# Gates, convolutions, the trigonometric table and statistics behind weight preparation, and a second work queue for the gates

## Chip, cores and metric

The kernel runs on one core of a Trainium2 chip. The metric is the device time of one execution in microseconds; the number quoted is the median of three runs.

## What the reference computes

A trunk of two layers works on x of 256 rows and 2048 columns in float32. Every layer normalises x, multiplies it by a large input matrix, and runs two token mixers beside each other: an mLSTM with 4 heads, whose q and k go through a depthwise convolution of width 5, and a retention with 8 heads, whose q and k are rotated. Both are gated, projected, mixed and added to x.

```python
h = rmsnorm(x, norm_w)
proj = jnp.einsum('bsd,de->bse', h, w_in)
qk_m = jax.nn.silu(depthwise_conv(jnp.concatenate([q_m, k_m], axis=-1), conv_w, conv_b))
gates = (g_m + b_mgate).reshape(b, s, 4, NH_M)
h_m = mlstm_scan(q_m, k_m, v_m, gates[0], gates[1]) + flipped(...)
q_r = rope(q_r, cos, sin);  k_r = rope(k_r, cos, sin)
h_r = retention_scan(...) + flipped(...)
y = mix_m * (u_m @ w_proj_m) + mix_r * (u_r @ w_proj_r)
return x + y @ w_out
```

## The kernel before

**Matrix products.** Every operand in float32 is split into a high and a low part (`hi`, `lo`), and a product is three matmuls (`mm3`). A `gemm` makes a block of 512 columns (384 or 400 for the first four blocks of q and k) for both halves of the rows. It walks over the 2048 inner elements in 8 chunks; a chunk loads 512 KB of weights into a tile `raw` (7 of them), splits them (`wsplit`: `whi` by a cast on ScalarE, `wlo` by a subtraction on VectorE; 12 tiles, so six chunks) and issues 12 matmuls into two PSUM tiles.

**Order of the blocks in a layer.** Five blocks of q and k for the mLSTM (qk0 with the 16 gate columns, qk1, qk2, qk3 of 384 columns, qk4 of 512), four value blocks (here vm0 to vm3), eight blocks of the retention's q, k and v, then gated blocks and projections. From the third value block on, further products (`seven`) are worked off beside the blocks as "side items"; they need sums of the operand (`s_hi`, `s_lo`, made by `sums_of_operand`).

**Work between the chunks.** What follows a block is put into the list `pending` by `later`, and `gemm` calls `run_later` before each chunk from the second or third on, which takes one step of the list's first entry. Entries are generators that yield where a step ends:

- `conv_block`: transposes three or four columns blocks of q or k (PSUM tile `tr`), a ScalarE activation for the middle tap, four `scalar_tensor_tensor` on VectorE for the others (`conv`), a Silu, and the split into `qkm_hi` and `qkm_lo`.
- `mlstm_gates`: some ten small steps from `gates` to the log forget gates `lf` (Exp and Ln on ScalarE), sums along the rows by six small matmuls (`pc`), diagonal tiles `dg`, which for every head are broadcast by two matmuls (`pb`) and reduced to the weights `wt` and their row maxima.
- `late_setup` (layer 0 only): loads positions (`pos_i`), `freq` and `rp`, and makes the table of sines and cosines in about 90 VectorE steps of 128x128.
- `mlstm_matrix`, one per head: scores (`psc`), row sums, the scaled matrix `a_sb`, its transpose `at`; then `mlstm_out` (`po`).

**What sets the order on an engine.** The code's order is not that of the queues. A planner of the framework places each instruction by its position in the code less an offset, as soon as its inputs and its tiles are ready in the plan; each engine then runs its queue in that order. Weight loads and splits have an offset of `AHEAD` = 800 positions, and whatever goes through the wrappers `vec` and `sca` one of `URGENT` = 1600:

```python
vec, sca = Ahead(nc.vector), Ahead(nc.scalar)   # every call under high_priority(offset=URGENT)
```

Matmuls have none. In the profile all instructions that go through the wrappers have line 119.

**Tiles.** Tags share a number of tiles: PSUM 8 (`bank`), `t512` 7 (q/k blocks, `conv`, `dg`, `freq`, `ahi`, `a_sb` and others), `act` 8 (`wt`, the table's two `trig` tiles, `at`, the split value blocks `vm_hi` and `vm_lo`, the operand sums).

Of the kernel before, what the change touches and what calls it, by code (L numbers as in the profile page):

```python
# [61 lines left out]
def encoder_kernel(ctx: ExitStack, tc: tile.TileContext, x, x_t, positions, w_main, w_qk0, w_qk1, b_mgate, vecs, b_mix,  # L62
# [92 lines left out]
    def late_setup():  # L155
        pos_i = sm.tile([P, NT], I32, name="pos_i", bufs=1)
        with nc.allow_non_contiguous_dma(reason="256 positions onto partitions"):
            nc.sync.dma_start(out=pos_i, in_=positions.rearrange("b (t p) -> p (b t)", p=P))
        freq = t512("freq")[:, 0:64]
        nc.sync.dma_start(out=freq, in_=inv_freq.broadcast_to([P, 64]))  # L160
        rp = sm.tile([P, 8], F32, name="rp", bufs=1)
        nc.sync.dma_start(out=rp, in_=rpieces.broadcast_to([P, 8]))
        pos_f = sm.tile([P, NT], F32, name="pos_f", bufs=1)
        vec.tensor_copy(out=pos_f, in_=pos_i)

        scr = [actt("trig0"), actt("trig1")]
        used = []

        def trig(name):
            used.append(name)  # L170
            i, n = divmod(len(used) - 1, 8)
            return scr[i][:, n * NT * 64:(n + 1) * NT * 64]
        ang = trig("ang")
        for t in range(NT):
            vec.tensor_scalar(out=ang[:, t * 64:(t + 1) * 64], in0=freq, scalar1=pos_f[:, t:t + 1],
                                    scalar2=None, op0=ALU.mult)
        ahi = t512("ahi", F32R)[:, 0:NT * 64]
        vec.tensor_copy(out=ahi, in_=ang)
        ahf = ahi.bitcast(F32)
        alo = trig("alo")  # L180
        vec.tensor_tensor(out=alo, in0=ang, in1=ahf, op=ALU.subtract)
        acc = trig("acc")
        vec.memset(acc, 0.0)


        def drop_turns(v, magic):
            rnd = trig("rnd")
            vec.tensor_scalar(out=rnd, in0=v, scalar1=magic, scalar2=magic, op0=ALU.add, op1=ALU.subtract)
            vec.tensor_tensor(out=v, in0=v, in1=rnd, op=ALU.subtract)
        for k in range(4, -1, -1):  # L190
            for part in (alo, ahf):
                del used[3:]
                pr = trig("pr")
                vec.tensor_scalar(out=pr, in0=part, scalar1=rp[:, k:k + 1], scalar2=None, op0=ALU.mult)
                drop_turns(pr, 1.5 * 2 ** 25)
                drop_turns(pr, 1.5 * 2 ** 23)
                vec.tensor_tensor(out=acc, in0=acc, in1=pr, op=ALU.add)
                drop_turns(acc, 1.5 * 2 ** 23)
        lim = 0.49999997
        vec.tensor_scalar(out=acc, in0=acc, scalar1=lim, scalar2=-lim, op0=ALU.min, op1=ALU.max)  # L200
        red = trig("red")
        vec.tensor_scalar(out=red, in0=acc, scalar1=6.283185307179586, scalar2=None, op0=ALU.mult)
        sca.activation(out=sin_sb, in_=red, func=AF.Sin)
        neg = trig("neg")
        vec.tensor_scalar(out=neg, in0=red, scalar1=-1.0, scalar2=None, op0=ALU.mult)
        vec.tensor_tensor(out=neg, in0=neg, in1=red, op=ALU.min)
        vec.tensor_scalar(out=neg, in0=neg, scalar1=1.5707963267948966, scalar2=None, op0=ALU.add)
        sca.activation(out=cos_sb, in_=neg, func=AF.Sin)
# [170 lines left out]
    def sums_of_operand(ht_hi, ht_lo, make_items):  # L379
        s_hi, s_lo = bigt("s_hi", 2, F32R), bigt("s_lo", 3, F32R)  # L380

        def whole(dst, kt):
            ks = slice(kt * S, (kt + 4) * S)
            vec.tensor_tensor(out=dst, in0=ht_hi[:, ks].bitcast(F32), in1=ht_lo[:, ks].bitcast(F32), op=ALU.add)
            return dst.rearrange("p (k t x) -> p k t x", t=NT, x=P)
        for j in range(2):
            a0 = whole(actt("a0"), 4 * j)
            a1 = whole(actt("a1"), HK + 4 * j)
            yield
            sums = [actt("sa"), actt("sb")]  # L390
            f = [s.rearrange("p (i k x) -> p i k x", i=2, x=P)[:, i] for s in sums for i in range(2)]
            vec.tensor_tensor(out=f[0], in0=a0[:, :, 1, :], in1=a1[:, :, 1, :], op=ALU.subtract)
            vec.tensor_tensor(out=f[1], in0=f[0], in1=a0[:, :, 0, :], op=ALU.subtract)
            vec.tensor_tensor(out=f[2], in0=a0[:, :, 0, :], in1=a0[:, :, 1, :], op=ALU.subtract)
            vec.tensor_tensor(out=f[3], in0=a1[:, :, 0, :], in1=f[1], op=ALU.add)
# [111 lines left out]
    def mlstm_gates(gates, gate_out):  # L507
# [6 lines left out]
        for t in range(NT):  # L514
            vec.tensor_copy(out=fpre[:, t], in_=g4[:, t, :, 1, :])
            vec.tensor_copy(out=ipre[:, t], in_=g4[:, t, :, 0, :])
        e, u, lf = small("e"), small("u"), small("lf")
        vec.scalar_tensor_tensor(out=e, in0=fpre, scalar=-1.0, in1=fpre, op0=ALU.mult, op1=ALU.max)
        sca.activation(out=e, in_=e, func=AF.Exp, scale=-1.0)
        vec.tensor_scalar(out=u, in0=e, scalar1=1.0, scalar2=None, op0=ALU.add)  # L520
        sca.activation(out=lf, in_=u, func=AF.Ln)
        d1 = small("d1")
        vec.tensor_scalar(out=d1, in0=u, scalar1=-1.0, scalar2=None, op0=ALU.add)
        vec.tensor_tensor(out=d1, in0=e, in1=d1, op=ALU.subtract)
        vec.reciprocal(out=u, in_=u)
        vec.tensor_tensor(out=d1, in0=d1, in1=u, op=ALU.mult)
        vec.tensor_tensor(out=lf, in0=lf, in1=d1, op=ALU.add)
        vec.scalar_tensor_tensor(out=lf, in0=fpre, scalar=0.0, in1=lf, op0=ALU.min, op1=ALU.subtract)
# [11 lines left out]
        vec.tensor_copy(out=cum, in_=pcv)  # L540
        vec.tensor_tensor(out=rj, in0=ipre, in1=cum, op=ALU.subtract)
# [8 lines left out]
        vec.tensor_copy(out=rj_hi, in_=rj)  # L550
        vec.tensor_tensor(out=rj_lo, in0=rj, in1=rj_hi.bitcast(F32), op=ALU.subtract)
# [3 lines left out]
        def diagonals(h):  # L555
            dgs = []
            for part in (rj_hi.bitcast(F32), rj_lo):
                dg = t512("dg", F32R)
                r = part[:, :, :, h:h + 1].rearrange("p t d o -> p d t o").broadcast_to([P, 2, NT, P])
                vec.tensor_tensor(out=dg.rearrange("p (d t x) -> p d t x", d=2, t=NT), in0=eye, in1=r,  # L560
                                        op=ALU.mult)
                dgs.append(dg)
            return dgs
        dgs = diagonals(0)
        for h in range(NH_M):
# [7 lines left out]
            for d, t, off, j0, nj, mask in pieces:  # L573
                w_h = wts[h][:, off:off + nj * P]
                vec.tensor_tensor_reduce(out=w_h, in0=pb[:, d * S + j0 * P:d * S + (j0 + nj) * P], in1=mask,
                                               scale=1.0, scalar=0.0, op0=ALU.add, op1=ALU.max,
                                               accum_out=rmax[:, t, d, h:h + 1])
        vec.tensor_scalar(out=nrm, in0=rmax, scalar1=-1.0, scalar2=None, op0=ALU.mult)
        for h in range(NH_M):
            for d, t, off, j0, nj, mask in pieces:  # L580
                w_h = wts[h][:, off:off + nj * P]
                sca.activation(out=w_h, in_=w_h, func=AF.Exp, bias=nrm[:, t, d, h:h + 1])
        floor = small("floor")
        vec.tensor_tensor(out=floor, in0=cum, in1=rmax, op=ALU.add)
        sca.activation(out=floor, in_=floor, func=AF.Exp, scale=-1.0)
        vec.tensor_scalar(out=floor, in0=floor, scalar1=16.0, scalar2=None, op0=ALU.mult)
# [3 lines left out]
    def conv_block(l, ch0, nch, ev, qk_hi, qk_lo):  # L590
        for g in range(0, nch, 2):
# [8 lines left out]
            for k2 in range(ng):  # L600
# [153 lines left out]
    for l in range(DEPTH):  # L754
# [6 lines left out]
        for b in range(5):  # L761
            if b == 0:
                ps = gemm(xop, wqk(w_qk0[l], N_QK0), "qk", N_QK0,
                          **(dict(ahead=first_raw, before=first_chunks) if l == 0 else dict(lead=2)))
                if l == 0:
                    for c in range(NBLK):
                        for t in range(NT):
# [3 lines left out]
                            sca.activation(out=xc, in_=xc, func=AF.Square,  # L771
# [206 lines left out]
        if l < DEPTH - 1:  # L978
# [164 lines left out]
```

## Time and profile before

| what | value |
|---|---|
| median of three runs | 2217.68 us (2213.07, 2217.68, 2217.74) |
| profiled execution: its own time | 2213.89 us |
| profiled execution: span | 2212.1 us, 28345 instructions |
| TensorE matmul busy | 2163.4 us (98%) |
| VectorE busy | 1766.4 us (80%) |
| ScalarE busy | 1269.7 us (57%) |
| DMA | 505.66 MB, mean 229 GB/s |

The profile is one execution; its times run from the start of the span. PE is TensorE (matmuls), PEld its weight loads, DVE VectorE, ACT ScalarE, POOL GpSimd, SP the engine that issues most DMAs. A name such as `wlo<-raw,whi` gives the tile written and the tiles read, and L119 is a line of the kernel. "PEclk" is the granted clock of TensorE as a share of full speed. Matmuls overlap each other, so the step from one start to the next, not the duration, is what one costs.

### The profile page before, as it was taken

The numbers are of one execution on the slowest core, as the hardware profiler recorded it, in microseconds if no ns is written. First come the engines' busy times: TensorE is split into PE (matmuls) and PEld (weight loads), VectorE is DVE, ScalarE is ACT, GpSimd is POOL, SyncE is SP. The second block draws the span as 40 slices with busy tenths as digits, with TensorE's granted clock in tenths as the row PEclk, the third lists the DMA queues.
The fourth block names the chain that finished last, engine by engine and source line by source line (L and its number), as shares of the span: only waits on it lengthen the run. The fifth ranks groups of instructions, "written<-read, shape, count | busy, mean of one in ns | idle before, by whom it ended". The sixth has DMA issues, their size and how long they took to land.

```text
span 2212.1 us, 28345 instructions
## 1 busy us (share of the span) xinstructions
PE 2163.4 (98%) x10072; PEld 1823.8 (82%) x10072; DVE 1766.4 (80%) x2281; ACT 1269.7 (57%) x1573; POOL 58.1 (3%) x114
## 2 busy tenths in 40 slices
PE   7889999999999999999999999999999999999998
PEld 6778888888788888888899888888888888888887
DVE  6895898888899879865568768889889988898654
ACT  7644556565766556654557445555567755666443
POOL 0000000000000000000000000000000000000000
PEclk9999999999999999999999999999999999999999
DMA  7455567667778877786756456666777788777763
GB/s 269 138 187 162 190 222 234 226 226 235 245 258 272 294 257 257 231 302 206 232 157 211 152 176 210 229 227 230 235 234 260 259 277 273 263 250 264 268 202 125
DMA packets 156190, 505.66 MB, mean 229 GB/s; under 512 B 18960, under 2 KB 21264, under 8 KB 156048
## 3 DMA queue, kind: packets, MB, share of 16 engines
q1 hardware_dynamic: 140240, 464.00, 63.4%
q0 software_dynamic: 8320, 27.27, 3.1%
q10 hardware_dynamic: 7488, 12.59, 2.0%
q8 instruction: 79, 1.29, 0.2%
q14 instruction: 63, 0.52, 0.1%
HBM read 474.42 MB, written 29.36 MB: 228 GB/s over the span
## 4 chain that ended last, share of the span: by engine, by line
PE 91%; DVE 4%; DMA 2%; ACT 1%; issue 1%; SPq 0%; ACTq 0%; DVEq 0%
PE pj L271 5%; PE pj L269 5%; PE pj L270 5%; PE wo L271 3%; PE wo L270 3%; PE vr L269 3%; PE vr L270 3%; PE wo L269 3%; PE vr L271 3%; PE qr L269 3%; PE zr L269 3%; PE zr L271 3%; PE qr L271 3%; PE qr L270 3%; PE zr L270 3%; PE vm L269 2%
## 5 line engine op out<-in xcount | busy, mean ns | idle before, releaser
L260 ACT CAST whi<-raw 128x1024 fp32r<-128x1024 f32 (+2 forms) x824 | 842.5, 1035 | 635.7 <-PE pj L270 119.7
L261 DVE TENSOR_TENSOR wlo<-raw,whi 128x1024 fp32r<-128x1024 f32 (+2 forms) x824 | 974.1, 1200 | 280.0 <-ACT whi L260 250.1
L269 PE MATMUL pj<-whi,u_hi 128*128 128x512 f32 x512 | 200.2, 391 | 0.0
L271 PE MATMUL pj<-whi,u_lo 128*128 128x512 f32 x512 | 199.4, 389 | 0.0
L270 PE MATMUL pj<-wlo,u_hi 128*128 128x512 f32 x512 | 199.3, 389 | 0.0
L260 ACT CAST whi<-keep 128x1024 fp32r<-128x1024 f32 x96 | 100.9, 1051 | 82.2 <-PE vr L270 19.1
L261 DVE TENSOR_TENSOR wlo<-keep,whi 128x1024 fp32r<-128x1024 f32 x96 | 117.1, 1219 | 28.8 <-ACT whi L260 27.6
L270 PE MATMUL qk<-wlo,ht_hi 128*128 128x384 f32 (+2 forms) x320 | 114.2, 357 | 13.3 <-DVE wlo L261 13.3
L269 PE MATMUL qk<-whi,ht_hi 128*128 128x384 f32 (+2 forms) x320 | 112.8, 357 | 11.6 <-ACT whi L260 11.6
L266 DVE TENSOR_TENSOR raw<-raw 128x1024 f32<-128x1024 f32 x96 | 117.0, 1218 | 0.8
L271 PE MATMUL qk<-whi,ht_lo 128*128 128x384 f32 (+2 forms) x320 | 113.3, 354 | 0.0
L271 PEld LDWEIGHTS pj<-whi,u_lo 128*128 128x128 f32 x512 | 96.1, 188 | 20.0
L270 PEld LDWEIGHTS pj<-wlo,u_hi 128*128 128x128 f32 x512 | 96.2, 188 | 19.6
L269 PEld LDWEIGHTS pj<-whi,u_hi 128*128 128x128 f32 x512 | 96.1, 188 | 19.6
L270 PE MATMUL zm<-wlo,ht_hi 128*128 128x512 f32 x256 | 100.1, 391 | 0.5 <-DVE wlo L261 0.5
L269 PE MATMUL vm<-whi,ht_hi 128*128 128x512 f32 x256 | 100.4, 392 | 0.0
L269 PE MATMUL vr<-whi,ht_hi 128*128 128x512 f32 x256 | 100.2, 392 | 0.0
L269 PE MATMUL zr<-whi,ht_hi 128*128 128x512 f32 x256 | 100.2, 391 | 0.0
L270 PE MATMUL vm<-wlo,ht_hi 128*128 128x512 f32 x256 | 100.2, 391 | 0.0
L269 PE MATMUL zm<-whi,ht_hi 128*128 128x512 f32 x256 | 100.1, 391 | 0.0
L269 PE MATMUL qr<-whi,ht_hi 128*128 128x512 f32 x256 | 100.1, 391 | 0.0
L271 PE MATMUL vm<-whi,ht_lo 128*128 128x512 f32 x256 | 100.0, 391 | 0.0
(294 smaller groups left out, 4651.1 us busy)
## 6 DMA issues: line engine op xcount, KB each, us to landing
raw<-in_w_main_dram SPq DMA_DIRECT2D x768, 512.0 KB, 5.1
raw<-in_w_qk_dram SPq DMA_DIRECT2D x48, 384.0 KB, 3.5
bm<-in_b_mix_dram ACTq DMA_DIRECT2D x32, 256.0 KB, 4.9
raw<-in_w_qk_dram SPq DMA_DIRECT2D x16, 400.0 KB, 5.6
hm<-hm POOLq DMA_DIRECT2D x16, 256.0 KB, 3.9
om<-c POOLq DMA_DIRECT2D x16, 256.0 KB, 5.1
hr<-hr POOLq DMA_DIRECT2D x16, 256.0 KB, 4.4
hm_b<-hm SPq DMA_DIRECT2D x16, 256.0 KB, 6.0
```

The costliest lines, as they stand in the source:

```text
L260: nc.scalar.copy(out=whi, in_=raw)
L261: nc.vector.tensor_tensor(out=wlo, in0=raw, in1=whi.bitcast(F32), op=ALU.subtract)
L266: nc.vector.tensor_tensor(out=dst, in0=a, in1=b, op=ALU.add)
L269: nc.tensor.matmul(out=ps, lhsT=xh, rhs=whi, start=first, stop=False)
L270: nc.tensor.matmul(out=ps, lhsT=xh, rhs=wlo, start=False, stop=False)
L271: nc.tensor.matmul(out=ps, lhsT=xl, rhs=whi, start=False, stop=last)
```

## The change

The convolutions, the gates, the table, the squares for the row statistics and the operand sums call the engines directly, so their instructions keep their place in the code (no offset). Evictions of PSUM, the rotation, `mlstm_matrix`, `rsqrt_mean` and all else that used the wrappers stay as they were. The gates and the table go into a list of their own, `beside`, and each call of `run_later` takes a step of `beside` and a step of `pending`. The table is queued one block earlier (b == 2) and cut into steps. A loop in front of the heads makes sure that the gates have been worked off.

```diff
     def late_setup():
...
-        vec.tensor_copy(out=pos_f, in_=pos_i)
+        nc.vector.tensor_copy(out=pos_f, in_=pos_i)
...
+        yield
         ang = trig("ang")
...
         for k in range(4, -1, -1):
+            yield
             for part in (alo, ahf):
...
-                vec.tensor_scalar(out=pr, in0=part, scalar1=rp[:, k:k + 1], scalar2=None, op0=ALU.mult)
+                nc.vector.tensor_scalar(out=pr, in0=part, scalar1=rp[:, k:k + 1], scalar2=None, op0=ALU.mult)
...
+    beside = []
+
     def run_later():
-        while pending:
-            try:
-                next(pending[0])
-                return
-            except StopIteration:
-                pending.pop(0)
+        for queue in (beside, pending):
+            while queue:
+                try:
+                    next(queue[0])
+                    break
+                except StopIteration:
+                    queue.pop(0)
...
     def sums_of_operand(ht_hi, ht_lo, make_items):
-            vec.tensor_tensor(out=dst, in0=ht_hi[:, ks].bitcast(F32), in1=ht_lo[:, ks].bitcast(F32), op=ALU.add)
+            nc.vector.tensor_tensor(out=dst, in0=ht_hi[:, ks].bitcast(F32), in1=ht_lo[:, ks].bitcast(F32), op=ALU.add)
...
-                split(hi, lo, src)
+                nc.scalar.copy(out=hi, in_=src)
+                nc.vector.tensor_tensor(out=lo, in0=src, in1=hi.bitcast(F32), op=ALU.subtract)
...
     def mlstm_gates(gates, gate_out):
-        sca.activation(out=e, in_=e, func=AF.Exp, scale=-1.0)
+        nc.scalar.activation(out=e, in_=e, func=AF.Exp, scale=-1.0)
...
-                vec.tensor_tensor(out=dg.rearrange("p (d t x) -> p d t x", d=2, t=NT), in0=eye, in1=r,
+                nc.vector.tensor_tensor(out=dg.rearrange("p (d t x) -> p d t x", d=2, t=NT), in0=eye, in1=r,
...
     def conv_block(l, ch0, nch, ev, qk_hi, qk_lo):
-                sca.activation(out=dst, in_=src, func=AF.Identity, scale=tap(2), bias=vcol(l, V_CB, ch))
+                nc.scalar.activation(out=dst, in_=src, func=AF.Identity, scale=tap(2), bias=vcol(l, V_CB, ch))
...
-                    vec.scalar_tensor_tensor(out=dst[:, d0:d1], in0=src[:, d0 + s:d1 + s], scalar=tap(w),
+                    nc.vector.scalar_tensor_tensor(out=dst[:, d0:d1], in0=src[:, d0 + s:d1 + s], scalar=tap(w),
...
-            sca.activation(out=acc, in_=acc, func=AF.Silu)
+            nc.scalar.activation(out=acc, in_=acc, func=AF.Silu)
...
-                            sca.activation(out=xc, in_=xc, func=AF.Square,
+                            nc.scalar.activation(out=xc, in_=xc, func=AF.Square,
...
             if b == 0:
-                later(mlstm_gates, gates, gate_out)
-            if l == 0 and b == 3:
-                later(late_setup)
+                beside.append(mlstm_gates(gates, gate_out))
+            if l == 0 and b == 2:
+                beside.append(late_setup())
...
         ats = {}
+        while not gate_out:
+            run_later()
...
     def x_stat(ev, b, ss):
-                    sca.activation(out=junk, in_=ev[t], func=AF.Square,
+                    nc.scalar.activation(out=junk, in_=ev[t], func=AF.Square,
```

In the code's order this moves the gates of a layer from the second to fourth block (qk1 to qk3) up to the second and third, the second convolution block from qk3 to qk2, and the table from qk4 to qk3 and the first chunks of qk4. The split at the end of `conv_block` still goes through the wrappers.

## Rows read from the trace of the kernel before

**Rows 1.** The page: busy time and share of the span, by engine.

```profile
PE 2163.4 (98%) x10072; PEld 1823.8 (82%) x10072; DVE 1766.4 (80%) x2281; ACT 1269.7 (57%) x1573; POOL 58.1 (3%) x114
```

**Rows 2.** Busy time by stretch: PE, PEld, DVE, ACT, POOL; clock; DMA.

```profile
30.00:50.00 20.00, 14.61 (x73) 12.59 (x72) 17.32 (x49) 16.28 (x23) 0.00 (x0) 0.84 0.46 154
90.00:110.00 20.00, 9.75 (x43) 8.05 (x42) 19.66 (x46) 15.18 (x26) 0.00 (x0) 0.74 0.18 54
150.00:170.00 20.00, 13.77 (x61) 11.82 (x60) 14.10 (x41) 9.82 (x16) 0.00 (x0) 0.74 0.46 157
35.00:155.00 120.00, 102.12 (x514) 91.51 (x512) 104.79 (x273) 71.70 (x110) 0.00 (x0) 0.93 0.49 160
...
1180.00:1200.00 20.00, 18.52 (x105) 17.63 (x104) 17.19 (x30) 17.17 (x30) 0.00 (x0) 1.00 0.45 138
1240.00:1260.00 20.00, 17.57 (x87) 14.90 (x86) 13.23 (x37) 8.97 (x15) 0.00 (x0) 0.91 0.44 153
```

**Rows 3.** Waits of TensorE, 0 to 170 us: total, times, longest.

```profile
PE qk L270 <- DVE wlo L261: 11.8, 4, 9.2
PE qk L269 <- ACT whi L260: 11.6, 3, 9.6
PE at L654 <- DVE a_sb L119: 6.2, 2, 3.4
PE pc L533 <- DVE lf L119: 1.5, 1, 1.5
```

**Rows 4.** Timeline of TensorE (PE): start, duration, line, tiles.

```profile
28.82 0.34 PE L269 MATMUL qk<-whi,ht_hi 128*128 128x384 f32 x1
...
33.72 0.33 PE L269 MATMUL qk<-whi,ht_hi 128*128 128x384 f32 x1
...
36.67 0.33 PE L271 MATMUL qk<-whi,ht_lo 128*128 128x384 f32 x1
...
165.19 0.63 PE L269 MATMUL vm<-whi,ht_hi 128*128 128x512 f32 x1
...
1155.78 0.39 PE L570 MATMUL pb<-dg,ones_r 128*128 128x512 f32 x1
...
1233.65 0.39 PE L270 MATMUL vm<-wlo,ht_hi 128*128 128x512 f32 x1
...
1241.82 0.40 PE L270 MATMUL vm<-wlo,ht_hi 128*128 128x512 f32 x1
```

**Rows 5.** Timeline of VectorE (DVE).

```profile
30.81 0.37 DVE L119 SCALAR_TENSOR_TENSOR gates<-qk,rstd,bg_sb 128x16 f32<-128x16 f32 x2
...
31.91 0.95 DVE L261 TENSOR_TENSOR wlo<-raw,whi 128x768 fp32r<-128x768 f32 x1
...
33.74 3.20 DVE L119 SCALAR_TENSOR_TENSOR conv<-tr,vec_sb,conv 128x254 f32<-128x254 f32 x8
...
44.63 0.68 DVE L119 TENSOR_TENSOR dg<-ident,rj_lo 128x512 fp32r<-128x512 f32 x1
...
148.87 1.21 DVE L261 TENSOR_TENSOR wlo<-raw,whi 128x1024 fp32r<-128x1024 f32 x1
...
164.31 0.74 DVE L119 SCALAR_TENSOR_TENSOR vm_lo<-vm,rstd,vm_hi 128x512 fp32r<-128x512 f32 x1
```

**Rows 6.** Timeline of ScalarE (ACT): a table load and what follows.

```profile
37.17 1.28 ACT L119 ACT_TABLE_LOAD   x1
38.46 0.42 ACT L119 ACTIVATE conv<-conv 128x256 f32<-128x256 f32 x1
```

**Rows 7.** Timeline of SyncE's DMA queue (SPq): two loads.

```profile
35.02 0.46 SPq L162 DMA_DIRECT2D rp<-in_rpieces_dram  x1
...
93.59 0.33 SPq L160 DMA_DIRECT2D freq<-in_inv_freq_dram  x1
```

**Rows 8.** Tiles s_lo and s_hi, 150 to 420 us: first and last start.

```profile
L119 DVE TENSOR_TENSOR s_lo<-sb,s_hi x2: 1212/1216/1219, 228.6 to 237.9; 128x1024 fp32r<-128x1024 f32 x2
...
L269 PE MATMUL sc<-whi,s_hi x14: 389/389/390, 262.1 to 417.6; 128*128 128x512 f32 x14
```

More of the change, by code (lines that the diff above doesn't have):

```diff
@@ L391, in sums_of_operand @@
             f = [s.rearrange("p (i k x) -> p i k x", i=2, x=P)[:, i] for s in sums for i in range(2)]
[L392 to L395, printed above, removed]
+            nc.vector.tensor_tensor(out=f[0], in0=a0[:, :, 1, :], in1=a1[:, :, 1, :], op=ALU.subtract)
+            nc.vector.tensor_tensor(out=f[1], in0=f[0], in1=a0[:, :, 0, :], op=ALU.subtract)
+            nc.vector.tensor_tensor(out=f[2], in0=a0[:, :, 0, :], in1=a0[:, :, 1, :], op=ALU.subtract)
+            nc.vector.tensor_tensor(out=f[3], in0=a1[:, :, 0, :], in1=f[1], op=ALU.add)
             yield
@@ L514, in mlstm_gates @@
         for t in range(NT):
-            vec.tensor_copy(out=fpre[:, t], in_=g4[:, t, :, 1, :])
-            vec.tensor_copy(out=ipre[:, t], in_=g4[:, t, :, 0, :])
+            nc.vector.tensor_copy(out=fpre[:, t], in_=g4[:, t, :, 1, :])
+            nc.vector.tensor_copy(out=ipre[:, t], in_=g4[:, t, :, 0, :])
         e, u, lf = small("e"), small("u"), small("lf")
-        vec.scalar_tensor_tensor(out=e, in0=fpre, scalar=-1.0, in1=fpre, op0=ALU.mult, op1=ALU.max)
-        sca.activation(out=e, in_=e, func=AF.Exp, scale=-1.0)
-        vec.tensor_scalar(out=u, in0=e, scalar1=1.0, scalar2=None, op0=ALU.add)
-        sca.activation(out=lf, in_=u, func=AF.Ln)
+        nc.vector.scalar_tensor_tensor(out=e, in0=fpre, scalar=-1.0, in1=fpre, op0=ALU.mult, op1=ALU.max)
+        nc.scalar.activation(out=e, in_=e, func=AF.Exp, scale=-1.0)
+        nc.vector.tensor_scalar(out=u, in0=e, scalar1=1.0, scalar2=None, op0=ALU.add)
+        nc.scalar.activation(out=lf, in_=u, func=AF.Ln)
         d1 = small("d1")
[L523 to L528, printed above, removed]
+        nc.vector.tensor_scalar(out=d1, in0=u, scalar1=-1.0, scalar2=None, op0=ALU.add)
+        nc.vector.tensor_tensor(out=d1, in0=e, in1=d1, op=ALU.subtract)
+        nc.vector.reciprocal(out=u, in_=u)
+        nc.vector.tensor_tensor(out=d1, in0=d1, in1=u, op=ALU.mult)
+        nc.vector.tensor_tensor(out=lf, in0=lf, in1=d1, op=ALU.add)
+        nc.vector.scalar_tensor_tensor(out=lf, in0=fpre, scalar=0.0, in1=lf, op0=ALU.min, op1=ALU.subtract)
         yield
@@ L539, in mlstm_gates @@
         cum, rj = small("cum"), small("rj")
-        vec.tensor_copy(out=cum, in_=pcv)
-        vec.tensor_tensor(out=rj, in0=ipre, in1=cum, op=ALU.subtract)
+        nc.vector.tensor_copy(out=cum, in_=pcv)
+        nc.vector.tensor_tensor(out=rj, in0=ipre, in1=cum, op=ALU.subtract)
         wts = [actt("wt") for _ in range(NH_M)]
@@ L549, in mlstm_gates @@
         rj_lo = small("rj_lo")
-        vec.tensor_copy(out=rj_hi, in_=rj)
-        vec.tensor_tensor(out=rj_lo, in0=rj, in1=rj_hi.bitcast(F32), op=ALU.subtract)
+        nc.vector.tensor_copy(out=rj_hi, in_=rj)
+        nc.vector.tensor_tensor(out=rj_lo, in0=rj, in1=rj_hi.bitcast(F32), op=ALU.subtract)
         eye = ident.rearrange("p (a b x) -> p a b x", a=1, b=1).broadcast_to([P, 2, NT, P])
@@ L581, in mlstm_gates @@
                 w_h = wts[h][:, off:off + nj * P]
-                sca.activation(out=w_h, in_=w_h, func=AF.Exp, bias=nrm[:, t, d, h:h + 1])
+                nc.scalar.activation(out=w_h, in_=w_h, func=AF.Exp, bias=nrm[:, t, d, h:h + 1])
         floor = small("floor")
-        vec.tensor_tensor(out=floor, in0=cum, in1=rmax, op=ALU.add)
-        sca.activation(out=floor, in_=floor, func=AF.Exp, scale=-1.0)
-        vec.tensor_scalar(out=floor, in0=floor, scalar1=16.0, scalar2=None, op0=ALU.mult)
+        nc.vector.tensor_tensor(out=floor, in0=cum, in1=rmax, op=ALU.add)
+        nc.scalar.activation(out=floor, in_=floor, func=AF.Exp, scale=-1.0)
+        nc.vector.tensor_scalar(out=floor, in0=floor, scalar1=16.0, scalar2=None, op0=ALU.mult)
         gate_out.extend((wts, floor, pieces))
```

32 lines of the change are left out of this document (16 added, 16 removed).

## Prediction

> **What bounds the kernel now.** I read the page first: TensorE is busy 2163.4 of 2212.1 us [rows 1], so no change that leaves its matmuls alone can give back more than the 49 us in which it stands idle, plus what a lowered clock costs. Then I asked for busy times by stretch, to find where those 49 us lie [rows 2]. Part of them lies before the first weights have arrived and behind the last matmul, out of the change's reach. In layer 0 three stretches stand out: 30 to 50 us (14.61 of 20 busy), 90 to 110 (9.75) and 150 to 170 (13.77): 21.9 us idle. The granted clock has means of 0.84, 0.74 and 0.74 there, so part of each ran at the lower level (1.2 GHz). I call them A, B and C. In layer 1 the same places lose 1.5 us (1180 to 1200) and 2.4 us (1240 to 1260, clock 0.91).
>
> Idle time and clock together come out of the timeline. The second block of q and k begins at 28.82 and the second value block (vm1) at 165.19 [rows 4]: 136.4 us. The pitch of a 384-column matmul is (36.67 - 33.72)/17 = 0.1735 us, of a 512-column one (1241.82 - 1233.65)/36 = 0.227 us [rows 4]. Between the two marks the code has 288 of the one (50.0 us) and 192 of the other (43.6 us), and about 11.7 us of transposes, scores and gate matmuls: 105.2 us. So A, B and C cost 31.2 us, of which 9.3 are lower clock.
>
> Then the waits of TensorE up to 170 us [rows 3]: 11.8 us for wlo and 11.6 for whi, the split weights; 6.2 for a_sb, a head's score matrix; 1.5 for lf, the gates. So A and B are late weights. VectorE is busy 19.66 of 20 us in B [rows 2], with convolutions, which carry an offset of 1600 and stand ahead of the weights' 800. C is another thing: the weights of vm1 are split from 148.87 on (to 150.1) [rows 5], yet vm1 begins at 165.19, behind the third head's scores, which the code asks for later. What ended just before is the eviction of the value block in front (164.31 plus 0.74) [rows 5].
>
> **Why C will not simply vanish.** My reading is that tiles of one tag are granted in the order in which the code asks for them. The `freq` load, on the shared t512 tag, is issued at 93.59, though `rp`, on a tag of its own and written beside it in the code, goes at 35.02 [rows 7]. In this reading vm1's second PSUM tile, eight behind the first of vm0, waits for vm0's eviction; that takes an act tile asked for behind head 0's transposed matrix; and that needs the fourth convolution block. So TensorE cannot run ahead of the convolutions by more than the value block under way, and vm1's start is a VectorE matter as well.
>
> **The change, part by part.** (1) Convolution, gate, table and operand-sum instructions lose the offset of 1600, so weight splits (800) go first wherever they have a tile. No instruction is added or removed. B's cause is gone: 10.2 us idle and its clock. A's two waits for weights go as well; its wait for lf (1.5 us) stays.
>
> (2) The gates run beside the convolutions: two steps a chunk instead of one. Before, the third q/k block (qk2) asked for its PSUM behind one convolution and the gates' cumulative sum; now the first two gate broadcasts (pb) come ahead of it as well. So qk2 waits until both are issued. TensorE, never stopped, ends qk1 at 28.82 + 96 x 0.1735 + 2.0 = 47.5. The chain of some 20 short dependent steps from `gates` to the first `dg` pair took 30.81 to 45.3 [rows 5], with eight convolution taps of 0.40 each (3.20/8) and more inside it. With those behind it, but weight splits of 0.9 ahead, I put the second pb at about 50: 3 us of wait, between 0 and 14 (every VectorE step of the chain finding one split in front).
>
> (3) VectorE up to vm1's start. It does the same work for that start as before, less the last convolution block, which need only have begun: 16 taps x 0.40 + 1.2 = 7.6 us. From 35 to 155 it was idle 120 - 104.79 = 15.2 us [rows 2], mostly while urgent work was not yet asked for; ahead-of-time gates and convolutions can fill that. I take two thirds (10 us) and 6 of the 7.6: 16 us, so vm1 at 149. Bounds: 0 if the order of steps keeps the gaps, 22.8 if all is filled. TensorE alone could be there at 165.2 - 31.2 + 3 = 137, so VectorE decides. The gain of (1) is not added to this: TensorE comes earlier to C and waits there longer.
>
> (4) The trigonometric table moves one block ahead and loses its offset. Its three loads stay in SP's queue. A `freq` load that waits for its tile holds the weight loads behind it; the seven raw tiles cover 7 x 2.08 = 14.6 us of that (12 matmuls of 0.1735 a chunk). I count 0; without the cover the wait falls on TensorE whole.
>
> (5) Statistics: eight squares of 0.6 us on ScalarE may slip behind casts, part of the chain in (2). The operand sums: s_lo is done at 239.1 and first read near 262 [rows 8]; 23 us of cover, cost 0. If it were gone, the products that read it would come later while other blocks run.
>
> (6) Table loads. Exp, Ln and Silu now alternate more: I allow four more loads of 1.28 us [rows 6] on ScalarE, which was idle 48 of the 120 us [rows 2]: 0, except two on the chain (2.6 us, inside (2)'s bounds). The Trainium skill ("ScalarE: Activation LUTs", What ACT_TABLE_LOAD costs) puts a switch at 2.66 us, 1.38 of it a drain. The trace shows no such drain: the activation behind the load of 37.17 starts 0.01 us after it ended [rows 6]. By the page the two would cost 5.3 us, still inside the bounds.
>
> (7) Layer 1 has no table, and VectorE is less full (17.19 and 13.23 of 20) [rows 2]. What it may win is the idle time of 3.9 us and about 2 of clock; what it may lose is (2): its first pb came at 1155.78 [rows 4], and the new order wants two by about the same time. I take 0, between -16 and +6.
>
> **Sum.** 16 us from 2213.89, the profiled execution's own time (its span and 1.8 us around it), gives 2198. The three runs have a mean of 2216.2, 2.3 above that execution, and a median of 2217.68: as a time of runs I forecast 2200.
>
> **Rivals.** *Nearly all comes back.* If tiles are not granted in order, TensorE goes on with vm1 and vm2: 28 us in layer 0 and up to 6 in layer 1, 2182 (2179 to 2191). For it: VectorE has slack from 170 us on. Against it: `freq`, and vm1's late start with its weights ready.
>
> *The wait only moves to C.* TensorE loses nothing in A and B, arrives early and waits for the same VectorE chain, because table work (now ahead of the fourth convolution) takes the gaps: 0 to 8 us gained, 2208 to 2216. For it: VectorE is nearly full from 90 us on. Against it: the 15.2 us of gaps lie earlier, when two convolution blocks could already run. The Trainium skill ("Perfetto Trace Analysis", Optimization Strategy) has a rule of this kind: repeated bubbles on the busiest engine can mean that no memory is free for the next tile. The trace bears it out at vm1, not at A and B, where weights ended the waits.
>
> *Slower.* The gate chain, now behind the splits in both layers, comes 10 us later than I count in layer 0 and 16 late in layer 1, with qk2 waiting: 2198 + 10 + 16 + 2.3 = 2226. It decides once the two delays exceed the 16 us of gain. For it: some 20 links, each of which can meet a split of 0.9. Against it: a split takes 0.95 us [rows 5] of the 2.08 that a chunk lasts, once the weight tiles are full, and in layer 0 VectorE works on through such a wait.
>
> **Chances and range.** VectorE-bound gain (2191 to 2208): 0.52. Nearly all: 0.16. Wait moves: 0.18, of which 0.06 faster than the bound. Slower: 0.12; 0.02 is left for no change at all. A run can tell 0.2% (4.4 us) from no change: faster 0.52 + 0.16 + 0.06 = 0.74, same 0.14, slower 0.12. The range, 2183 to 2219, leaves out the slower case and a part of the best.
>
> **What the profile after will show.** Right: from 90 to 110 TensorE busy throughout at clock 1.00; splits of weights between single convolution taps; qk2 behind two pb; VectorE over 95% busy from 50 to 130; one wait of TensorE of some 10 us before vm1, which starts near 149. Wrong: vm1 before 140 (tiles not in order), or after 160 (gaps not filled); qk2 more than 8 us behind qk1; new idle time behind 200 us or in layer 1.

## The result and the profile after

| kernel | median, us | profiled execution, us | its span, us |
|---|---|---|---|
| before (4 runs beside it) | 2215.47 | 2213.89 | 2212.1 |
| after (4 runs) | 2190.76 (2188.10 to 2191.61) | 2188.10 | 2186.4 |

The ratio of after to before is 0.9887, 95% interval [0.9869, 0.9904]: 24.7 us or 1.1% faster. Forecast were 2200 us, with a range from 2183 to 2219.

The page of the changed kernel, busy time by engine, to be set beside [rows 1]:

```profile
PE 2155.9 (99%) x10072; PEld 1815.6 (83%) x10072; DVE 1766.3 (81%) x2281; ACT 1267.1 (58%) x1572; POOL 58.3 (3%) x114
```

The same work but for one load of an activation table, in a span 25.7 us shorter. Busy time by stretch, columns as in [rows 2]:

```profile
30.00:50.00 20.00, 18.46 (x111) 17.94 (x112) 16.73 (x37) 14.20 (x20) 0.00 (x0) 1.00 0.77 255
50.00:70.00 20.00, 15.96 (x83) 15.16 (x82) 19.12 (x49) 10.48 (x18) 0.00 (x0) 0.91 0.41 121
70.00:90.00 20.00, 20.00 (x120) 19.93 (x119) 14.90 (x37) 15.56 (x28) 0.00 (x0) 1.00 0.69 228
90.00:110.00 20.00, 20.00 (x95) 16.82 (x94) 18.52 (x39) 14.22 (x23) 0.00 (x0) 1.00 0.64 215
110.00:130.00 20.00, 20.00 (x99) 16.88 (x98) 19.62 (x58) 11.37 (x17) 0.00 (x0) 1.00 0.55 185
130.00:150.00 20.00, 20.00 (x104) 16.65 (x103) 19.09 (x65) 10.52 (x15) 0.00 (x0) 1.00 0.40 131
150.00:170.00 20.00, 18.83 (x90) 14.78 (x88) 19.45 (x59) 9.88 (x15) 0.00 (x0) 1.00 0.55 184
35.00:155.00 120.00, 115.76 (x608) 103.84 (x607) 107.94 (x282) 72.64 (x111) 0.00 (x0) 0.99 0.57 185
1180.00:1200.00 20.00, 20.00 (x93) 16.59 (x92) 18.02 (x30) 14.31 (x21) 0.00 (x0) 1.00 0.58 196
1240.00:1260.00 20.00, 20.00 (x92) 16.48 (x91) 10.92 (x13) 9.47 (x13) 1.10 (x2) 1.00 0.50 167
```

B (90 to 110) has gone from 9.75 us busy to 20.00, at full clock. C (150 to 170) has gone from 13.77 to 18.83. A has only moved: 30 to 50 is better filled than before, and 50 to 70, full before, has a hole of 4 us with a lowered clock. The two stretches of layer 1 are full.

Waits of TensorE from 0 to 170 us, for [rows 3]; the longest wait for whi, 9.2 us, stands at the start of the kernel, as one of 9.6 us does before (TensorE's first matmul there starts at 9.56 us):

```profile
PE qk L271 <- ACT whi L262: 9.4, 2, 9.2
PE pb L576 <- DVE dg L566: 4.0, 1, 4.0
PE qk L272 <- DVE wlo L263: 1.4, 1, 1.4
PE po L379 <- ACT vm_hi L119: 1.2, 1, 1.2
```

Behind that start the waits for late weights are down to 1.6 us (1.4 for wlo, 0.2 for whi), those for a_sb are gone, and one for the diagonal tiles `dg` is new. TensorE's timeline, for [rows 4]: the end of the first gate broadcast, the last matmul of qk1, the second broadcast, the first matmul of qk2, and the start of vm1:

```profile
46.60 0.42 PE L576 MATMUL pb<-dg,ones_r 128*128 128x512 f32 x1
...
50.50 0.34 PE L273 MATMUL qk<-whi,ht_lo 128*128 128x384 f32 x1
54.88 1.31 PE L576 MATMUL pb<-dg,ones_r 128*128 128x512 f32 x2 [4.04 <-DVE dg L566]
55.98 0.52 PE L271 MATMUL qk<-whi,ht_hi 128*128 128x384 f32 x1
...
142.10 0.39 PE L271 MATMUL vm<-whi,ht_hi 128*128 128x512 f32 x1
```

VectorE between the two broadcasts, for [rows 5]:

```profile
45.78 0.68 DVE L566 TENSOR_TENSOR dg<-ident,rj_lo 128x512 fp32r<-128x512 f32 x1
46.39 0.99 DVE L617 SCALAR_TENSOR_TENSOR conv<-tr,vec_sb,conv 128x254 f32<-128x254 f32 x2
...
52.48 1.65 DVE L617 SCALAR_TENSOR_TENSOR conv<-tr,vec_sb,conv 128x255 f32<-128x255 f32 x4
54.05 0.68 DVE L566 TENSOR_TENSOR dg<-ident,rj_hi 128x512 fp32r<-128x512 f32 x1
```

The second pair of diagonals stands behind twelve convolution taps and three weight splits, and TensorE stands at the broadcast meanwhile, 4.04 us. The clock falls behind that wait; columns as in [rows 2]:

```profile
54.88:57.90 3.02, 3.02 (x8) 2.67 (x9) 2.87 (x12) 2.45 (x6) 0.00 (x0) 0.50 0.08 28
```

To compare many kernels I count what a stretch loses: its length less the number of matmuls that begin in it times their undisturbed step (0.1735 and 0.227 us for 384 and 512 columns [rows 4], 0.18 for 400 and about 0.11 for narrower ones). That holds idle time and lowered clock together, to about half a us. A is 29 to 90 us, B 90 to 110, C 110 to 190, L1 1140 to 1260.

```
us lost in     A      B      C     L1
before        9.0   12.4   10.5    6.6
after         8.0    0.4    2.6    0.7
```

B gives 12.0, C 7.9, layer 1 5.9, A 1.0: 26.8 against 25.7 of span; the rest of the kernel loses about 1 us more.

### The profile page after: what moved, and what is told of

It reads as the page before. It is cut to its first block, busy times and chain, and to the rows that moved or that the text cites. A ratio compares the mean times of both kernels' runs of the same rounds, so it can differ in the third digit from the quotient of the medians.

```text
span 2186.4 us, 28371 instructions
## 1 busy us (share of the span) xinstructions
PE 2155.9 (99%) x10072; PEld 1815.6 (83%) x10072; DVE 1766.3 (81%) x2281; ACT 1267.1 (58%) x1572; POOL 58.3 (3%) x114
## 4 chain that ended last, share of the span: by engine, by line
PE 94%; DMA 2%; DVE 2%; ACT 1%; issue 1%; SPq 0%; ACTq 0%; DVEq 0%
PE pj L273 5%; PE pj L272 5%; PE pj L271 5%; PE wo L271 3%; PE wo L273 3%; PE vr L272 3%; PE vr L271 3%; PE wo L272 3%; PE zr L273 3%; PE qr L271 3%; PE qr L272 3%; PE qr L273 3%; PE zr L272 3%; PE vr L273 3%; PE zr L271 3%; PE vm L271 3%
## 5 line engine op out<-in xcount | busy, mean ns | idle before, releaser
L272 PE MATMUL vr<-wlo,ht_hi 128*128 128x512 f32 x256 | 99.8, 390 | 0.0
```

Of the source, the lines that this page charges most:

```text
L272: nc.tensor.matmul(out=ps, lhsT=xh, rhs=wlo, start=False, stop=False)
```

## The experiments

All ratios are to the kernel before, run beside them. Losses are in the table at the end of this section.

**Convolutions alone.**

> The kernel before with one part of the change: the convolutions' Identity, taps and Silu keep their place in the code (no offset of 1600); one queue as before, gates, table and sums urgent as before. Theory (the convolutions' offset is the whole cost): weights are ready in the stretch 90 to 110, the value block vm0 starts about 12 us earlier than in the kernel before and vm1 about 20, the time is 2190 to 2196, as with the whole change. Rival (the second queue and the unhurried table are what frees the stretch around 150 to 170): vm0 gains its 12 us, vm1 gives most of it back, the time is 2201 to 2206.

```diff
-                sca.activation(out=dst, in_=src, func=AF.Identity, scale=tap(2), bias=vcol(l, V_CB, ch))
+                nc.scalar.activation(out=dst, in_=src, func=AF.Identity, scale=tap(2), bias=vcol(l, V_CB, ch))
...
-                    vec.scalar_tensor_tensor(out=dst[:, d0:d1], in0=src[:, d0 + s:d1 + s], scalar=tap(w),
+                    nc.vector.scalar_tensor_tensor(out=dst[:, d0:d1], in0=src[:, d0 + s:d1 + s], scalar=tap(w),
...
-            sca.activation(out=acc, in_=acc, func=AF.Silu)
+            nc.scalar.activation(out=acc, in_=acc, func=AF.Silu)
```

Measured: 2194.78 us, ratio 0.9906 [0.9891, 0.9921]. The time is the theory's, but the places are not: A, B and layer 1 lose next to nothing (vm0 starts at 108.9, 19 us before the kernel before), and C loses 14.2. Its waits from 30 to 170 us:

```profile
PE psc L374 <- ACT qkm_hi L119: 5.9, 2, 5.4
PE at L654 <- DVE a_sb L119: 4.4, 2, 4.0
PE qk L270 <- DVE wlo L261: 1.1, 2, 0.8
```

The weights are on time; scores now wait for convolved q and k. Without the convolutions' offset B, layer 1's losses and, with the single queue, nearly all of A are gone. C has another cause.

**The second queue alone.**

> The kernel before with the other part alone: the second queue for gates and table, the table one block earlier, and every wrapper of 1600 as before. Theory (offsets decide, the order of asking does not): the waits for whi and wlo between 90 and 110 stay, the time is within 5 us of the kernel before, 2211 to 2221. Rival (asking earlier fills VectorE's gaps before 90 us, so urgent work no longer piles up in front of the splits): 8 to 15 us faster, 2201 to 2208.

```diff
+    beside = []
...
+        for queue in (beside, pending):
...
-                later(mlstm_gates, gates, gate_out)
-            if l == 0 and b == 3:
-                later(late_setup)
+                beside.append(mlstm_gates(gates, gate_out))
+            if l == 0 and b == 2:
+                beside.append(late_setup())
```

Measured: 2215.88 us, ratio 0.9999 [0.9991, 1.0008]: no change. Inside, it is not the same kernel: B has gone (asking earlier does spread the work, as the rival had it), but A loses 12.3, C 14.3 and layer 1 9.4. Waits from 30 to 170 us:

```profile
PE qk L272 <- DVE wlo L263: 7.3, 4, 4.3
PE at L659 <- DVE a_sb L119: 6.8, 2, 4.0
PE pb L575 <- DVE dg L119: 2.6, 2, 1.7
```

In time the theory holds, in place neither does: weights are still late, 4.3 us at 68.6 and 2.1 at 116.8 instead of in B, so the losses change places.

**The changed kernel with an urgent table.**

> The changed kernel with the trigonometric table's steps urgent again (offset 1600), all else as changed. Theory (the late table, which ends at 168 us on VectorE, holds back the evictions of vm0 and vm1 and costs the 2.9 us that vm2 gives back): the evictions come before 160 us, vm2 starts 2 to 3 us earlier than in the changed kernel, 2187 to 2189. Rival (some 90 urgent steps of about 0.2 us stand in front of weight splits again): TensorE waits 5 to 10 us for wlo between 70 and 110 us, 2195 to 2201.

```diff
-                nc.vector.tensor_scalar(out=pr, in0=part, scalar1=rp[:, k:k + 1], scalar2=None, op0=ALU.mult)
+                vec.tensor_scalar(out=pr, in0=part, scalar1=rp[:, k:k + 1], scalar2=None, op0=ALU.mult)
...
-                nc.vector.tensor_tensor(out=acc, in0=acc, in1=pr, op=ALU.add)
+                vec.tensor_tensor(out=acc, in0=acc, in1=pr, op=ALU.add)
```

(and so through the whole of `late_setup`). Measured: 2201.18 us, ratio 0.9931 [0.9917, 0.9944], slower than the changed kernel by some 10 us. The time is just above the rival's range and the rival's wait is wrong: not weights, but the third head's scores wait, and vm1 comes right behind them. TensorE's timeline:

```profile
148.05 0.58 PE L379 MATMUL psc<-qkm_hi 128*128 128x256 f32 x1 [6.50 <-ACT qkm_hi L119]
148.43 0.63 PE L271 MATMUL vm<-whi,ht_hi 128*128 128x512 f32 x1
```

So the table's offset is the second part that counts: some 22 us of VectorE work (30 steps of 0.28, 30 of 0.22 and 30 more of about that size) that stands, when urgent, before the last convolutions.

**The changed kernel with urgent gates.**

> The changed kernel with the gates' steps urgent again, all else as changed. Theory (the second gate broadcast waits 4.0 us because convolution taps and weight splits stand before the diagonal tiles on VectorE): the broadcasts wait less than 1 us in layer 0 and layer 1, 3 to 5 us faster than the changed kernel, 2185 to 2188. Rival (the gates then stand before the splits and the weights come late in the same place): the wait turns into one for wlo or whi, the time stays within 2 us of the changed kernel or rises to 2195.

```diff
-                nc.vector.tensor_tensor(out=dg.rearrange("p (d t x) -> p d t x", d=2, t=NT), in0=eye, in1=r,
+                vec.tensor_tensor(out=dg.rearrange("p (d t x) -> p d t x", d=2, t=NT), in0=eye, in1=r,
```

(and so through the whole of `mlstm_gates`). Measured: 2189.89 us, ratio 0.9888 [0.9872, 0.9903]: the same as the changed kernel. The wait for `dg` is gone and A loses 3.9 instead of 8.0, as the theory has it, but C takes most of it back, 5.8 instead of 2.6; the time is the rival's, its wait for weights is not what came. From 30 to 170 us its longest wait is a new one:

```profile
PE po L379 <- DVE at L119: 2.9, 1, 2.9
```

**One act tile for the table.** Behind the table's sine (167.33 us) all of ScalarE's casts and evictions of this stage come at once in the changed kernel; its ScalarE timeline:

```profile
167.33 0.31 ACT L205 ACTIVATE sin_sb<-trig 128x128 f32<-128x128 f32 x1 [1.75 <-DVE trig L204]
167.55 1.06 ACT L119 CAST at<-at 128x512 fp32r<-128x512 f32 x2
168.49 1.28 ACT L119 ACTIVATE vm_hi<-vm,rstd 128x512 fp32r<-128x512 f32 x2
```

though TensorE had transposed head 0 at 131.2. The gates' weights (four) and the table (two) hold six of the eight act tiles. Two runs take one of the table's two away, from the changed kernel and (below) from one that waits longer there.

> The changed kernel with the table's scratch in one act tile instead of two (the cosine's argument takes a slot that is free by then). Theory (the evictions of vm0 and vm1 and the casts of the transposed matrices come only at 167.5 to 171.9 us, right behind the table's sine, because the eight act tiles are all taken): the casts and evictions spread over 130 to 160 us, and vm2 starts up to 2.9 us earlier than in the changed kernel, 2187 to 2189. Rival (VectorE, busy 95 to 98% of 110 to 170 us with the same steps, sets the start of vm2): the evictions come early, but vm2 starts within 1 us of the changed kernel, 2189 to 2192.

```diff
-        scr = [actt("trig0"), actt("trig1")]
+        scr = [actt("trig0")]
...
+        del used[3:]
         red = trig("red")
```

Measured: 2194.36 us, ratio 0.9891 [0.9875, 0.9908]: no gain, and slower than both expectations. The first casts and the eviction of vm0 do come early (133.5, 140.8, 142.6), so the tiles held them; but TensorE comes to the third head's scores at 143.2 and waits 2.8 us for the convolution, and C loses 5.1.

**The table late.**

> The changed kernel with the table queued behind the second value block (its scratch in the sine and cosine tiles and in one t512 tile, no act tile). Theory (VectorE sets vm2's start, and the table's some 18 us of steps are its only work there that nobody needs before 240 us): vm2 starts 5 to 12 us earlier than in the changed kernel, the wait of 4.0 us for the diagonal tiles stays, 2179 to 2186. Rival (the later convolutions and heads bind, not the table): vm2 within 3 us of the changed kernel, 2188 to 2191. Worse (the table now holds up the evictions or the operand sums between 190 and 240 us): new waits behind 190 us, 2192 or more.

```diff
+        acc, ang = (z.rearrange("p t i -> p (t i)") for z in (sin_sb, cos_sb))
...
+        own = t512("ahi", F32R)
+        ahi, alo, pr, rnd = (own[:, n * NT * 64:(n + 1) * NT * 64] for n in range(4))
...
-            if l == 0 and b == 2:
-                beside.append(late_setup())
...
             later(mlstm_out, l, b, ats, vm)
+            if l == 0 and b == 1:
+                beside.append(late_setup())
```

Measured: 2191.10 us, ratio 0.9878 [0.9864, 0.9893]: the same as the changed kernel. Busy time by stretch:

```profile
50.00:70.00 20.00, 15.97 (x79) 15.20 (x78) 18.23 (x48) 10.45 (x16) 0.00 (x0) 0.83 0.41 108
130.00:150.00 20.00, 20.00 (x105) 16.93 (x105) 18.38 (x51) 13.91 (x22) 0.00 (x0) 1.00 0.47 145
150.00:170.00 20.00, 20.00 (x99) 16.73 (x98) 11.21 (x26) 8.32 (x11) 1.23 (x2) 1.00 0.52 171
```

Taking the table away empties VectorE (11.21 of 20 instead of 19.45) and gives TensorE back 2.3 of the 2.6 us that it still lost in C, no more, since there was no more; vm2 starts at 172.05, in the changed kernel at 172.55. My theory fell, and the time is the rival's: but for these 2.3 us VectorE no longer sets vm2's start in the changed kernel, TensorE's own work does. No new wait came between 190 and 400 us. A loses 2.4 us more here than in the changed kernel, ahead of the table's steps; why is not shown.

**Convolutions and table, one queue.**

> The kernel before with convolutions and table without their offset; one queue, gates urgent, table in its old place. Theory (convolutions and table explain layer 0, the second queue costs 6 us ahead of vm0 and 2 us in layer 1 and gives nothing back): vm0 near 109, vm2 at 171 to 173, time 2187 to 2190, at or slightly below the changed kernel. Rival (the second queue's earlier gates are needed to have the first heads ready): vm2 at 176 or later, 2193 to 2197.

The edit is that of the first run, and `nc.vector` and `nc.scalar` throughout `late_setup`, in its old place. Measured: 2191.75 us, ratio 0.9884 [0.9869, 0.9898]: level with the changed kernel, by other places. A loses 1.7, C 12.8; vm2 comes at 176.8, which is the rival's number. ScalarE's timeline and TensorE's wait:

```profile
169.93 0.31 ACT L203 ACTIVATE sin_sb<-trig 128x128 f32<-128x128 f32 x1 [7.12 <-DVE trig L202]
170.15 1.05 ACT L119 CAST at<-at 128x512 fp32r<-128x512 f32 x2
171.09 1.28 ACT L119 ACTIVATE vm_hi<-vm,rstd 128x512 fp32r<-128x512 f32 x2
...
171.84 1.22 PE L374 MATMUL po<-vm_hi,at 128*128 128x512 f32 x2 [9.88 <-ACT vm_hi L119]
```

The stack behind the sine is as late as in the changed kernel, but TensorE, 6 us earlier at vm0, has run out of other work. With one act tile for the table:

> The kernel with convolutions and table without offset (one queue, table in its old place), and the table's scratch in one act tile instead of two. Theory (the 9.9 us in which the first outputs wait for vm_hi come from the act tiles: the casts of the transposed matrices and the evictions get no tile in the planner's order before the table is done, and so stand behind the sine in ScalarE's queue): at casts and vm_hi come between 125 and 160 us, the wait of po for vm_hi is gone, the loss from 150 to 190 us falls from 12.6 to below 5, 2183 to 2188. Rival (the late table itself holds ScalarE's queue, whatever the tiles): the wait stays above 5 us, 2190 to 2193.

The edit of the run with one act tile, on top of the run before. Measured: 2186.62 us, ratio 0.9862 [0.9843, 0.9881]. ScalarE's timeline:

```profile
129.68 0.57 ACT L119 CAST at<-at 128x512 fp32r<-128x512 f32 x1
...
137.49 1.27 ACT L119 ACTIVATE vm_hi<-vm,rstd 128x512 fp32r<-128x512 f32 x2
...
182.47 0.31 ACT L204 ACTIVATE sin_sb<-trig 128x128 f32<-128x128 f32 x1 [3.40 <-DVE trig L203]
```

The sine is later still and nobody waits for it: with a tile to be had, the casts stand in front of it in ScalarE's queue, and the wait of 9.9 us is gone. The rival's wait did not come, and the time is the theory's; the intervals of the two kernels overlap. From 150 to 190 us 0.6 us are lost instead of 12.6; ahead of that, 130 to 150 now loses 6.3, as the scores wait 3.3 us for qkm_hi again.

**Statistics.**

> The changed kernel with the squares of the row statistics and the operand sums urgent again. Theory (covered work, the term was put at 0): within 2 us of the changed kernel, 2189 to 2193, no loss of TensorE behind 190 us in another place. Rival (the operand sums' ten or so long VectorE steps stand before splits between 190 and 240 us, and the unhurried squares had made room on ScalarE at the start): 2194 or more, with waits for wlo between 190 and 240 us.

```diff
-                            nc.scalar.activation(out=xc, in_=xc, func=AF.Square,
+                            sca.activation(out=xc, in_=xc, func=AF.Square,
...
-                nc.scalar.copy(out=hi, in_=src)
-                nc.vector.tensor_tensor(out=lo, in0=src, in1=hi.bitcast(F32), op=ALU.subtract)
+                split(hi, lo, src)
```

(and the other five lines of sums and squares). Measured: 2191.45 us, ratio 0.9891 [0.9872, 0.9909]: level with the changed kernel within the 4 us that such an interval leaves. Its trace shows nothing lost behind 190 us; in A it shows 13.6 us lost instead of 8.0, with the wait for `dg` at 5.2 and one for whi of 2.2. Kernels whose work up to 70 us is that of the changed one lose 8.0, 8.2, 9.7 and 10.4 there, so a part of the 13.6 may be the squares; the times do not show it.

**The remedies together.**

> The kernel before with convolutions without their offset, gates urgent in the one queue, and the table alone in a queue beside, behind the second value block, as in the run before last. Theory (both remaining losses go: the wait for the diagonal tiles and the table's share of VectorE ahead of vm2): vm0 near 109, vm2 at 160 to 166, layer 1 as with the convolutions alone, 2177 to 2183, the fastest of all. Rival (heads and convolutions alone fill VectorE up to vm2): vm2 near 171, 2186 to 2189.

The edits are those of the first run and of the late table; `beside` holds the table alone. Measured: 2188.26 us, ratio 0.9866 [0.9852, 0.9881]. A loses 1.8, layer 1 nothing, vm2 comes at 168.5, between the theory's 166 and the rival's 171, and the time is the rival's; C loses 4.3, as the third head's scores wait 2.8 us for qkm_hi and the granted clock is 0.91 from 130 to 150 us.

> The kernel with convolutions without offset and the table beside, late (one queue for gates and convolutions), and three empty steps ahead of the third head. Theory (its one wait between 70 and 240 us, 2.8 us of the third head's scores for the last convolution block and the lowered clock behind it, 4.6 us in all, comes from asking for the scores too early): the wait goes, 2183 to 2186. Rival (the wait only moves to the outputs of a value block, which then come before their transposed matrix): a wait of po for at or vm_hi of 2 to 5 us, 2187 to 2190.

```diff
         for h in range(NH_M):
+            if l == 0 and h == 2:
+                later(pause, 3)
             later(mlstm_matrix, h, ats, qk_hi, qk_lo, gate_out)
```

Measured: 2181.32 us (2179.09 to 2181.97), ratio 0.9842 [0.9827, 0.9857], the fastest, better than its theory, and clear of the changed kernel's interval. Its stretches:

```profile
50.00:70.00 20.00, 20.00 (x115) 19.73 (x115) 18.95 (x48) 11.30 (x16) 0.00 (x0) 1.00 0.64 190
...
130.00:150.00 20.00, 20.00 (x98) 16.76 (x97) 16.25 (x33) 11.54 (x16) 0.00 (x0) 1.00 0.50 169
150.00:170.00 20.00, 20.00 (x99) 16.84 (x98) 13.95 (x31) 10.64 (x15) 0.69 (x1) 1.00 0.49 166
```

The scores were only asked for too early; asked for later, nothing waits in their place. The gain on the kernel before it in this list is 6.9 us, of which 4.0 lie in C; the two intervals overlap a little. Another 1.4 us are a wait of TensorE for a rotated block (`ro`) between 190 and 400 us, which the trace of the kernel before it has and this one has not; the rest is not traced.

> The changed kernel with the gates urgent again and the table late. Theory (the two losses of the changed kernel in layer 0, some 8 us from 29 to 70 us and 2.5 us from 130 to 170, have separate causes and their cures add up): 29 to 70 us loses about 4, 130 to 170 less than 1, time 2184 to 2188. Rival (TensorE that comes earlier out of the first stretch runs into the last convolution block, as it did with the single queue): a wait of the scores for qkm_hi of 2 to 6 us, 2188 to 2192.

The edits are those of the urgent gates and of the late table. Measured: 2182.84 us, ratio 0.9848 [0.9833, 0.9864]. The theory holds by place, and the time is 1 us below its range: A loses 3.5, C 0.5. Either cure alone was worth nothing measurable (2189.89 and 2191.10), both together about 8 us.

```
us lost in                        A      B      C     L1    median
before                          9.0   12.4   10.5    6.6   2215.47
after                           8.0    0.4    2.6    0.7   2190.76
convolutions alone              1.9    0.1   14.2    0.0   2194.78
second queue alone             12.3   -0.1   14.3    9.4   2215.88
after, table urgent             8.2    0.1    9.6    2.1   2201.18
after, gates urgent             3.9    0.5    5.8    0.2   2189.89
after, one act tile             9.7    0.3    5.1    2.0   2194.36
after, table late              10.4    0.1    0.3    1.2   2191.10
convolutions and table          1.7    0.1   12.8    0.4   2191.75
the same, one act tile          1.8    0.1    7.1    0.2   2186.62
after, statistics urgent       13.6    0.2    2.7    1.2   2191.45
convolutions, table late        1.8    0.1    4.3    0.0   2188.26
the same, third head later      2.3    0.1    0.3    0.4   2181.32
after, gates urgent, t. late    3.5    0.1    0.5    0.5   2182.84
```

## Why the prediction was right, and where its steps were not

The direction and the range were right, the cause of B was right, and the size was 9 us short: layer 0 gave some 5 us more than forecast, under (3), layer 1 some 6, under (7), and the rest of the kernel lost about 1. The picture of what would bind afterwards was wrong: a kernel bound by VectorE just before vm1, with a wait of some 10 us, did not come, and TensorE waits for nothing from 70 to 150 us. VectorE was to be over 95% busy from 50 to 130; from 70 to 90 it is busy 14.90 of 20 us. By the steps:

**(1) Offsets and weights.** Right at B: 12.0 us came back, and with the convolutions alone B is gone. The 11.6 us for whi in [rows 3] were misread: 9.6 of them are the kernel's first wait, ahead of A, and B's 10.2 us are 9.17 for wlo and 1.08 for whi, by TensorE's timeline of the kernel before:

```profile
9.56 1.03 PE L269 MATMUL qk<-whi,ht_hi 128*128 128x400 f32 x2 [9.56 <-ACT whi L260]
...
94.42 0.73 PE L269 MATMUL qk<-whi,ht_hi 128*128 128x512 f32 x2 [1.08 <-ACT whi L260]
...
104.97 0.80 PE L270 MATMUL qk<-wlo,ht_hi 128*128 128x512 f32 x1 [9.17 <-DVE wlo L261]
```

In A 3.7 us of waits for weights became 1.6, so that part was right as well; what A keeps is another wait. With the convolutions' offset gone and one queue, A loses 1.9 us; the changed kernel keeps 8.0, for the reason of (2).

**(2) The gates beside.** Forecast: 3 us of wait, between 0 and 14, for the second broadcast at about 50. Measured: 4.0 us of wait for a broadcast at 54.88. The mechanism was right, and qk2 did wait until both broadcasts were issued: qk1's last matmul starts at 50.50, qk2's first at 55.98. The broadcast came 5 us later than counted and qk1 ended 3 us later, which leaves a wait only 1 us longer. I left out the clock: from 54.88 to 57.90 it was granted at 0.50 (1.2 GHz), and with that the stretch from 50 to 60 loses 5.9 us. In all the second queue and the unhurried gates cost 6.1 us in A (8.0 less 1.9), so A gave back 1 us of its 9.0. I had looked for single splits in front of the chain; twelve convolution taps stood there too, which had lost the same offset.

**(3) vm1 at 149, a gain of 16 us.** This is the term that was mis-sized most: vm1 came at 142.10, 23.1 us earlier, beyond even the upper bound of 22.8. The failing sentence is "it does the same work for that start as before, less the last convolution block". The table's 22 us lost their offset as well, so the heads could pass them on VectorE, and they went on until 168. VectorE from 35 us to vm1's start, whole and for the table's `trig` tiles alone; first the kernel before, then the changed one:

```profile
35.00:165.19 130.19, 108.73 (x546) 97.83 (x545) 111.30 (x292) 75.12 (x116) 0.00 (x0) 0.90 0.49 165
35.00:142.10 107.10, 102.86 (x545) 92.94 (x543) 95.69 (x242) 66.99 (x104) 0.00 (x0) 0.98 0.58 189
...
35.00:165.19 130.19, 20.77 (x90) 0.90 0.49 165
35.00:142.10 107.10, 11.89 (x50) 0.98 0.58 189
```

VectorE worked 15.6 us less, 8.9 of them table steps, and was idle 11.4 us instead of 18.9: the gaps gave 7.5 us, not 10, and the table, which was put at nothing, gave 8.9. Where the table stays urgent both terms come out near the forecast: 7.2 us idle, so 11.7 of gaps filled, 5.1 us less work, vm1 at 148.43 and 2201.18 us, against 149 and 2200. The path there is another one, though: vm1 waits behind the third head's scores, not for vm0's eviction. In the changed kernel VectorE no longer decides: TensorE is at full rate from 70 to 150 us, and taking the table away altogether gives 2.3 us in C and nothing measurable in the time. TensorE alone was put at 137, with 3 us of wait in A; A loses 8.0, and 137 and 5 make the 142 that was measured. So there is some luck in the size: two misses of opposite sign stand in it, 5 us too little loss counted in A and no gain counted for the table.

**Tiles in the order of the code.** This reading falls for vm1 in the changed kernel: it starts at 142.10, and the block before it is evicted only at 168.49, so no PSUM tile waited for that eviction. For the kernel before, where vm1 does start right behind the eviction, it stays open; all of the 6.2 us that TensorE stood idle in C there are its two waits for a_sb. `freq` was no proof of it: its load still goes long after that of `rp` (75.47 against 49.13), and what holds it back is not shown. The narrower claim, that act tiles hold up evictions, does hold, and costs 9.9 us of wait in one kernel and 1.2 in the changed one. The Trainium skill ("Perfetto Trace Analysis", Optimization Strategy) says that repeated bubbles on the busiest engine can mean that no memory is free for the next tile. The runs with one act tile agree on the cause, though the wait here was a single one of 9.9 us: with one queue the first cast came 40 us earlier (129.68 against 170.15) and the wait was gone, once a tile was free.

**(4), (5), (6) at nothing.** The loads of the table cost nothing. The operand sums, which now run from 202 to 222 us, cost nothing: TensorE waits for nothing from 170 to 240. The squares stay open within 4 us. ScalarE's table loads did not rise by four: up to 130 us there are seven, one fewer than before, as no Silu now stands between the gates' Exp and Ln, as one did at 38.46 [rows 6]. One of 1.28 us stands at 35.63 in the gate chain and the activation behind it starts at 36.92, 0.01 us after it.

**(7) Layer 1 at nothing.** It gave 5.9 us, the upper bound, so this term was mis-sized too. With the convolutions alone the waits of 1.5 us for wlo and 2.4 for a_sb are gone, and 6.6 us come back; the second queue with everything urgent costs 2.8. The late broadcasts that I feared wait 0.8 us in all.

**Rivals.** "Nearly all comes back", given a chance of 0.16, was right in B, layer 1 and most of C and wrong in A; the measured 2190.76 lies just inside its range and just outside that of the favoured case, and its 2182 us is what the two best kernels reach. "The wait only moves to C" did not happen in the changed kernel, but it did in five of the others: where A loses under 4 us, C loses 4 to 14, unless the table is late and q and k are convolved by the time the third head's scores are asked for. The slower case had the right chain: its broadcast came 5 us later than counted in layer 0, not 10, and in layer 1 it cost next to nothing.

## What to carry to other kernels

When a part loses its priority, ask not only what goes ahead of it but what else has lost it too: work that nobody needs for another 70 us (the table) leaves the path, and work that somebody waits for (the gates) falls behind its neighbours. Of two waits in a row on one engine, a cure of the first can lengthen the second: urgent gates alone took 4.1 us out of A and C rose by 3.2. Neither cure alone showed a gain, and both together gave 8 us, so a cure that shows none alone may still be worth keeping for the next. Count losses by place, since equal times can hide opposite changes.

## What the runs showed of the hardware

A short wait of TensorE can cost more than itself: behind the 4.04 us at the gate broadcast the granted clock was 0.50 (1.2 GHz) from 54.88 to 57.90, and the stretch from 50 to 60 us loses 5.9 us in all. Nothing else was unexpected: table loads of 1.28 us without a pause behind them, as in [rows 6].
